# VectorE's arithmetic of gathered expert rows ordered behind the one-hot products, and 92 in place of 100 expert tiles run ahead

## The chip, the cores and the metric

The kernel runs on one core of a Trainium2 chip. The metric is the device time of one execution in microseconds (us); three executions are shown, and the median is what counts. One more execution was recorded by the profiler, and all rows and sums below are of that one.

## What is computed

One decoder layer over 512 tokens of 1024 features: a chunked gating mixer and a sparse attention, merged and added to the input, and then a feed-forward layer of 16384 single-neuron experts (128 x 128 keys). The change touches this last part alone:

```python
sub = jnp.einsum('bshpd,hpnd->bshpn', q, subkeys)       # 8 heads, 2 x 128 keys
s_top, i_top = lax.top_k(sub, PEER_TOPK)                # 16 of each half
...
best, pos = lax.top_k(cand, PEER_TOPK)                  # 16 experts of a head
gate = jax.nn.softmax(best, axis=-1)
...
ub = u_tab[eb]                                          # 128 experts of a token
vb = v_tab[eb]
a = jax.nn.gelu(jnp.einsum('td,ted->te', xb, ub))
return jnp.einsum('te,ted->td', (gb * a).astype(vb.dtype), vb)
```

All arrays are float32.

## The kernel before

The 512 tokens are four blocks of 128. The first three blocks (384 tokens, the **dense** way) are computed against all 16384 experts by matmul, with gates that are zero for the experts a token did not choose. The fourth block (the **sparse** way) fetches the 128 chosen rows of each token from memory.

**Dense, first half.** The u table is 128 tiles of 128 experts. `expert_in` (L652) loads a tile (`load_w`, L81: a DMA of 512 KB on SP's queue into `wraw`, 3 buffers; ScalarE rounds it into `whi`, L86; VectorE takes the rest `wlo`, L87) and makes 24 matmuls into `pa` (8 chunks, three products each, L91 to L93, 384 columns); ScalarE's gelu evacuates it. The first 28 results stay on chip; tiles from `KEPT` = 28 to `AHEAD` are written to memory (`ad`, L660) and read back later (L900).

**Dense, gates.** `choose` (L755) finds each token's experts. For each block, 16 steps of 8 tokens then build the gate matrix out of one-hot products: four VectorE operations of 128x1024 (`jb`, `ib`, `o1`, `o2`, L837 to L840), 16 small matmuls into `pg` (L846), an evacuation by ScalarE into `ch`, and a write to memory (`gd`, L850, one for two steps). There are 48 such steps.

**Dense, second half.** For each of 128 tiles of the v table (L888 on): the tile is loaded like the u tiles, a slice of the gates is read back (`gg`, 1.5 MB for 8 tiles), VectorE multiplies the activations by the gates (`pr`, L904), ScalarE and VectorE split the product (`ph`, `pl`), and 18 matmuls of 512 columns add into six banks `y`.

**Sparse.** `sparse_in` (L672) gathers one chosen u row for each of the 128 tokens (GpSimd issues an indirect DMA of 512 KB into `gt`, L668, **three buffers**), and one VectorE operation (L674) multiplies by the token's features and sums; every 16 of them a gelu and a multiplication make `coef`. `sparse_out` (L681) gathers a v row and VectorE adds it, weighted, to `h2l` (L683). There are 128 of each; a gather can be issued when the VectorE operation three gathers earlier has freed its buffer.

**What sets the order.** The text runs `ahead(1)` (L687) before each one-hot step, an expert tile, and after every second tile a `sparse_in`; when the one-hot steps are through, `ahead(P)` does the tiles up to `AHEAD`. In the last loop `feed()` (L865) puts the rest of the sparse work evenly between the loads. But the order in which an engine executes is not the text's: when the program is built, a scheduler plays it through with durations of its own and lets an instruction go ahead of others on its engine when its operands are ready there. The executed order is fixed from then on, and each engine takes its instructions strictly in that order. `tc.issue_after(x)` forbids the scheduler to put what is inside ahead of `x`.

Of the kernel before, what the change touches and what calls it, by code (L numbers as in the profile page):

```python
# [15 lines left out]
ALU = mybir.AluOpType  # L16
# [44 lines left out]
def kernel(ctx: ExitStack, tc: tile.TileContext, x, pos, cst, wtok, wsm, wcol, wkv, spt,  # L61
                             wab, wo, wq, skt, g1b, g2b, u_rows, ut, v_rows, out, dbg=None):
    nc = tc.nc
    V, G, A, T, SY = nc.vector, nc.gpsimd, nc.scalar, nc.tensor, nc.sync
# [78 lines left out]
    with ExitStack() as c1:  # L143
# [39 lines left out]
        with tc.tile_pool(name="xin", bufs=4, reuse_waits="tile") as xp:  # L183
# [53 lines left out]
            with tc.tile_pool(name="rp", bufs=1) as rp:  # L237
# [38 lines left out]
                for k, p2 in ((a1, 9), (a2, 20)):  # L276
# [4 lines left out]
                    t = tmp()  # L281
                    V.tensor_scalar(t, k, mh, None, ALU.mult)
                    t = reduce(t)
                    t = sub_mul(t, k, -(m - mh))
# [87 lines left out]
        for b in range(NB):  # L372
# [8 lines left out]
            s = m  # L381
# [89 lines left out]
        for b in range(1, NB):  # L471
            s = madd[b]
# [20 lines left out]
        for g in range(4):  # L493
# [8 lines left out]
            t = sc.tile([P, S], F32, name="zt", tag="w", bufs=NW)  # L502
# [69 lines left out]
        h2l = spp.tile([P, D], F32, name="h2l")  # L572
# [8 lines left out]
        for p in range(4, 8):  # L581
            out_tile(p, ybh, ybl)
            for i in (2 * p - 8, 2 * p - 7):
                t = sg[i]
# [11 lines left out]
        hn3 = spp.tile([P, D], F32, name="hn3")  # L596
# [36 lines left out]
    TO = 8  # L633
    NCH = ND // TC
    JG = 8
    AHEAD = 100
    KEPT = 28
    EARLY = 2
    GS = 2.0 ** 15
# [3 lines left out]
    dots = spp.tile([P, P], F32, name="dots")  # L643
    coef = spp.tile([P, P], F32, name="coef")
# [21 lines left out]
    def gather(table, s):  # L666
# [2 lines left out]
                             in_offset=bass.IndirectOffsetOnAxis(ap=eid[:, s:s + 1], axis=0))  # L669
        return t  # L670

    def sparse_in(s):  # L672
        t = gather(u_rows, s)
        V.tensor_tensor_reduce(out=t, in0=t, in1=hn3, scale=1.0, scalar=0.0, op0=ALU.mult, op1=ALU.add,  # L674
                               accum_out=dots[:, s:s + 1])
        if s % PK == PK - 1:
            hs = slice(s - PK + 1, s + 1)
            A.activation(coef[:, hs], dots[:, hs], AF.Gelu_apprx_tanh)
            V.tensor_tensor(coef[:, hs], coef[:, hs], gate3[:, hs], ALU.mult)

    def sparse_out(s):  # L681
        t = gather(v_rows, s)
        V.scalar_tensor_tensor(h2l, t, coef[:, s:s + 1], h2l, ALU.mult, ALU.add)  # L683

    n_in = 0

# [9 lines left out]
    with ExitStack() as c2:  # L696
# [114 lines left out]
        for b in range(NB - 1):  # L811
            ahead(2)
            tr = []
            for n, src in enumerate(choose(b)):
                pt = sm.tile([P, S], F32, name="pgt", tag="sm")
                T.transpose(pt[:, :P], src, ident)
                t = gs.tile([P, P], F32 if n == 2 else F16, name=f"tr{n}")
# [5 lines left out]
            glo = gs.tile([P, P], F16, name="glo")  # L823
            V.tensor_tensor(glo, gT, ghi, ALU.subtract)
            for cc in range(P // TC):
                ch = chp.tile([P, P, TC], F32, name="ch")
                for to in range(0, TC, TO):
# [4 lines left out]
                    def over(a):  # L832
                        return (a[:, t0:t0 + TO].rearrange("p (g u) -> p g u", u=2).unsqueeze(2)
                                .to_broadcast([P, TO // 2, P, 2]))
# [2 lines left out]
                    V.tensor_tensor(jb, iob, over(jT), ALU.is_equal)  # L837
                    V.tensor_tensor(ib, iob, over(iT), ALU.is_equal)
                    V.tensor_tensor(o1, ib, over(ghi), ALU.mult)
                    V.tensor_tensor(o2, ib, over(glo), ALU.mult)  # L840
                    for t4 in range(0, TO, 4):
                        pg = gp.tile([P, 4, P], F32, name="pg")
                        for u in range(4):
# [148 lines left out]
```

## Time and profile before

| what | us |
|---|---|
| three executions | 1598.27, 1598.01, 1592.77 |
| median | 1598.01 |
| the profiled execution | 1593.43 |
| its span, first to last instruction | 1591.7 |
| TensorE busy in it | 1559.4 |
| VectorE busy | 1265.2 |
| ScalarE busy | 657.5 |
| GpSimd busy | 345.4 |

The profiled execution stands 4.6 us below the median of the three. TensorE's mean granted clock is 0.993 of full speed. Instructions of an engine overlap a little at their ends, so a mean duration is slightly more than the step from one start to the next; for matmuls the overlap is large, and the step is what counts. Up to about 450 us the profile shows the mixer and attention and then the query projections; from 530 to 890 us the gates and the expert tiles that run ahead; from there to the end the v tiles with the remaining u tiles.

### The profile page before, as it was taken

To read this page: it belongs to the slowest core of one execution; us is meant where nothing else is said; L and a number is where in the kernel's file an instruction comes from. 1 tells how busy PE (TensorE), PEld (TensorE's weight loads), DVE (VectorE), ACT (ScalarE), POOL (GpSimd) and SP (SyncE) were. 2 spreads that over 40 slices of the span, in tenths; PEclk is the share of its full clock that TensorE was granted. 3 is DMA by queue.
4 is the path that set the end of the run, shared out by engine and by line. 5 is a ranking of instruction groups with operands and counts; after the bars stand their busy time and mean duration, and the time that the engine had idled before them with its cause. 6 is when DMAs were issued, how large, how long until landed. Compare 5 with 4: busy or idle time off the path is not lost.

```text
span 1591.7 us, 22605 instructions
## 1 busy us (share of the span) xinstructions
PE 1559.4 (98%) x8173; PEld 1359.1 (85%) x8173; DVE 1265.2 (79%) x2648; ACT 657.5 (41%) x976; POOL 345.4 (22%) x280
## 2 busy tenths in 40 slices
PE   8998999999999999999999899999999999999998
PEld 6777767888899999899999898888888888888787
DVE  5599945557999999999999567788777788788764
ACT  5453453322335345455567343333333333333232
POOL 0010000000000454333222223343322223334300
PEclk9999999999999999999999999999999999999999
DMA  6211225222223789999999998899999999999862
GB/s 219 80 54 67 93 71 194 93 93 93 80 93 120 256 304 339 330 328 356 365 342 340 369 348 271 304 352 346 361 330 354 351 338 333 328 316 317 274 230 94
DMA packets 160416, 395.01 MB, mean 248 GB/s; under 512 B 12976, under 2 KB 80560, under 8 KB 156720
## 3 DMA queue, kind: packets, MB, share of 16 engines
q1 hardware_dynamic: 109616, 220.01, 39.6%
q0 software_dynamic: 36864, 134.23, 23.7%
q10 hardware_dynamic: 13824, 39.33, 6.4%
q8 instruction: 64, 1.05, 0.3%
q14 instruction: 48, 0.39, 0.1%
HBM read 350.53 MB, written 42.99 MB: 247 GB/s over the span
## 4 chain that ended last, share of the span: by engine, by line
PE 78%; DMA 9%; issue 6%; DVE 3%; POOL 2%; ACT 1%; SPq 0%; POOLq 0%; DVEq 0%; ACTq 0%
PE pa L93 9%; PE pa L91 9%; PE pa L92 9%; PE y L92 7%; PE y L93 7%; PE y L91 7%; DMA gt<-in_v_rows,eid 5%; PE pg L846 3%; POOL gt L668 2%; PE pcol L92 2%; PE pcol L91 2%; PE pcol L93 2%; PE pq L91 2%; PE pq L92 2%; PE pq L93 2%
## 5 line engine op out<-in xcount | busy, mean ns | idle before, releaser
L86 ACT CAST whi<-wraw 128x1024 fp32r<-128x1024 f32 x320 | 334.6, 1051 | 322.1 <-PE pa L92 127.0
L87 DVE TENSOR_TENSOR wlo<-wraw,whi 128x1024 fp32r<-128x1024 f32 x320 | 389.1, 1219 | 88.1 <-ACT whi L86 81.1
L91 PE MATMUL pa<-hh,whi 128*128 128x384 f32 (+2 forms) x1040 | 351.2, 338 | 10.0 <-ACT actd L659 10.0
L93 PE MATMUL pa<-hh,wlo 128*128 128x384 f32 (+2 forms) x1040 | 349.7, 337 | 1.1 <-DVE wlo L87 1.1
L92 PE MATMUL pa<-hl,whi 128*128 128x384 f32 (+2 forms) x1040 | 349.6, 336 | 0.0
L92 PE MATMUL y<-wlo,ph 128*128 128x512 f32 x768 | 302.3, 394 | 4.5 <-DVE wlo L87 4.5
L93 PE MATMUL y<-whi,pl 128*128 128x512 f32 x768 | 300.9, 393 | 0.0
L668 POOL DMA_INDIRECT gt<-in_u_rows,eid x128 | 177.9, 1390 | 527.9 <-DVE dots L674 308.8
L908 ACT CAST ph<-pr 128x384 fp32r<-128x384 f32 x128 | 65.8, 514 | 381.2 <-PE y L92 360.0
L668 POOL DMA_INDIRECT gt<-in_v_rows,eid x128 | 155.3, 1213 | 308.8 <-DVE h2l L683 276.3
L91 PEld LDWEIGHTS pa<-hh,whi 128*128 128x128 f32 x1040 | 196.5, 189 | 15.3 <-ACT actd L659 11.0
L91 PE MATMUL y<-whi,ph 128*128 128x512 f32 x768 | 207.6, 392 | 0.2 <-ACT ph L908 0.2
L93 PEld LDWEIGHTS pa<-hh,wlo 128*128 128x128 f32 x1040 | 196.3, 189 | 6.2 <-DVE wlo L87 2.2
L92 PEld LDWEIGHTS pa<-hl,whi 128*128 128x128 f32 x1040 | 196.6, 189 | 4.2
L683 DVE SCALAR_TENSOR_TENSOR h2l<-gt,coef,h2l 128x1024 f32<-128x1024 f32 x128 | 163.8, 1280 | 27.0 <-DMA gt<-in_v_rows,eid 26.2
L92 PEld LDWEIGHTS y<-wlo,ph 128*128 128x128 f32 x768 | 144.9, 189 | 34.9 <-DVE wlo L87 5.1
L93 PEld LDWEIGHTS y<-whi,pl 128*128 128x128 f32 x768 | 145.0, 189 | 28.4 <-DVE pl L909 0.3
L674 DVE CUSTOM_DVE_ANT_0 gt<-gt,hn 128x1024 f32<-128x1024 f32 x128 | 155.3, 1218 | 17.0 <-DMA gt<-in_u_rows,eid 16.9
L91 PEld LDWEIGHTS y<-whi,ph 128*128 128x128 f32 x768 | 143.7, 188 | 26.9 <-ACT ph L908 0.5
L909 DVE TENSOR_TENSOR pl<-pr,ph 128x384 fp32r<-128x384 f32 x128 | 71.2, 556 | 90.8 <-ACT ph L908 87.2
L848 ACT ACTIVATE ch<-pg 128x512 f32<-128x512 f32 x96 | 96.6, 1112 | 29.5 <-PE pg L846 29.5
L904 DVE TENSOR_TENSOR pr<-act,gg 128x384 f32<-128x384 f32 x128 | 70.7, 554 | 2.1
(304 smaller groups left out, 1930.4 us busy)
## 6 DMA issues: line engine op xcount, KB each, us to landing
wraw<-in_ut SPq DMA_DIRECT2D x128, 512.0 KB, 5.6
wraw<-in_v_rows SPq DMA_DIRECT2D x128, 512.0 KB, 6.6
gd<-ch ACTq DMA_DIRECT2D x24, 1024.0 KB, 6.3
gg<-gd SPq DMA_DIRECT2D x15, 1536.0 KB, 15.1
ad<-actd ACTq DMA_DIRECT2D x72, 192.0 KB, 5.5
act<-ad SPq DMA_DIRECT2D x72, 192.0 KB, 7.3
wraw<-in_wcol SPq DMA_DIRECT2D x20, 512.0 KB, 3.2
wraw<-in_wq SPq DMA_DIRECT2D x16, 512.0 KB, 3.2
```

The lines of the kernel that those rows point to most:

```text
L86: A.copy(hi, raw)
L87: V.tensor_tensor(lo, raw, hi.bitcast(F32), ALU.subtract)
L91: T.matmul(ps, lh, rh, start=start, stop=False)
L92: T.matmul(ps, lh, rl, start=False, stop=False)
L93: return T.matmul(ps, ll, rh, start=False, stop=stop)
L668: G.indirect_dma_start(out=t, out_offset=None, in_=table, in_offset=bass.IndirectOffsetOnAxis(ap=eid[:, s:s + 1], axis=0))
L674: V.tensor_tensor_reduce(out=t, in0=t, in1=hn3, scale=1.0, scalar=0.0, op0=ALU.mult, op1=ALU.add, accum_out=dots[:, s:s + 1])
L683: V.scalar_tensor_tensor(h2l, t, coef[:, s:s + 1], h2l, ALU.mult, ALU.add)
L848: A.activation(ch[:, :, to + t4:to + t4 + 4].rearrange("p i t -> p t i"), pg, AF.Copy, scale=1.0 / GS)
L904: V.tensor_tensor(pr.rearrange("p (c t) -> p c t", c=NCH), acts[j].rearrange("p (c t) -> p c t", c=NCH), gt[:, :, j % JG, :], ALU.mult)
L908: A.copy(ph, pr)
L909: V.tensor_tensor(pl, pr, ph.bitcast(F32), ALU.subtract)
```

## The change

The sparse VectorE operations (`sparse_in`'s product and `sparse_out`'s addition) may no longer be placed ahead of the last one-hot product `o2` that the text has emitted before them. Before the first one-hot step there is none, and they are free. `AHEAD` goes from 100 to 92: 8 expert tiles are done in the last loop instead of in front of it, 8 fewer results go through `ad`, and 4 fewer `sparse_in` stand in the text before the last loop.

```diff
--- before.py
+++ after.py
@@ -633,7 +633,7 @@
     TO = 8
     NCH = ND // TC
     JG = 8
-    AHEAD = 100
+    AHEAD = 92
     KEPT = 28
     EARLY = 2
     GS = 2.0 ** 15
@@ -669,10 +669,17 @@
                              in_offset=bass.IndirectOffsetOnAxis(ap=eid[:, s:s + 1], axis=0))
         return t
 
+    last_v = None
+
+    def paced():
+
+        return tc.issue_after(last_v.ins) if last_v is not None else nullcontext()
+
     def sparse_in(s):
         t = gather(u_rows, s)
-        V.tensor_tensor_reduce(out=t, in0=t, in1=hn3, scale=1.0, scalar=0.0, op0=ALU.mult, op1=ALU.add,
-                               accum_out=dots[:, s:s + 1])
+        with paced():
+            V.tensor_tensor_reduce(out=t, in0=t, in1=hn3, scale=1.0, scalar=0.0, op0=ALU.mult, op1=ALU.add,
+                                   accum_out=dots[:, s:s + 1])
         if s % PK == PK - 1:
             hs = slice(s - PK + 1, s + 1)
             A.activation(coef[:, hs], dots[:, hs], AF.Gelu_apprx_tanh)
@@ -680,7 +687,8 @@
 
     def sparse_out(s):
         t = gather(v_rows, s)
-        V.scalar_tensor_tensor(h2l, t, coef[:, s:s + 1], h2l, ALU.mult, ALU.add)
+        with paced():
+            V.scalar_tensor_tensor(h2l, t, coef[:, s:s + 1], h2l, ALU.mult, ALU.add)
 
     n_in = 0
 
@@ -837,7 +845,7 @@
                     V.tensor_tensor(jb, iob, over(jT), ALU.is_equal)
                     V.tensor_tensor(ib, iob, over(iT), ALU.is_equal)
                     V.tensor_tensor(o1, ib, over(ghi), ALU.mult)
-                    V.tensor_tensor(o2, ib, over(glo), ALU.mult)
+                    last_v = V.tensor_tensor(o2, ib, over(glo), ALU.mult)
                     for t4 in range(0, TO, 4):
                         pg = gp.tile([P, 4, P], F32, name="pg")
                         for u in range(4):
```

What becomes of the order is seen on VectorE's queue. Names: `gt,dots<-gt,hn` is `sparse_in`'s product (with a second row that reads out the sum), `h2l<-gt,coef,h2l` is `sparse_out`'s addition, `wlo` the split of any weight tile, `ib`, `jb` and `o` the one-hot products, the rest of the first place belongs to `choose`; `eid` holds the row numbers for the gathers. Line numbers of the change are 8 higher from L681 on.

The first place: VectorE from the first gathered product on, soon after `eid` is known. Before:

```order
L674 ISA gt,dots<-gt,hn_2653 128x1024
L674 ISA dots 128x1
L781 TENSOR_SCALAR qt_5560<-qa 128x128
L715 MATCH_REPLACE cand<-best,cand 128x64 x3
L87 TENSOR_TENSOR wlo<-wraw,whi 128x1024
L674 ISA gt,dots<-gt,hn_2653 128x1024
L674 ISA dots 128x1
L793 TENSOR_TENSOR eq<-eq 128x128x8
L716 MAX best<-cand 128x8
L674 ISA gt,dots<-gt,hn_2653 128x1024
L674 ISA dots 128x1
```

and with the change:

```order
L681 ISA gt,dots<-gt,hn_2653 128x1024
L681 ISA dots 128x1
L789 TENSOR_SCALAR qt_5560<-qa 128x128
L723 MATCH_REPLACE cand<-best,cand 128x64 x3
L87 TENSOR_TENSOR wlo<-wraw,whi 128x1024
L801 TENSOR_TENSOR eq<-eq 128x128x8
L724 MAX best<-cand 128x8 x5
L788 SCALAR_TENSOR_TENSOR qb<-qa,qb 128x128
L87 TENSOR_TENSOR wlo<-wraw,whi 128x1024
L724 MAX best<-cand 128x8 x3
L801 TENSOR_TENSOR eq<-eq 128x128x4
```

Before, a product follows every two or three rows of `choose`; now one is placed here, and the next comes 57 rows later, after the first `o2`.

The second place: VectorE from the last `o2` on. Before:

```order
L840 TENSOR_TENSOR o_7818<-ib,glo 128x1024
L87 TENSOR_TENSOR wlo<-wraw,whi 128x1024
L674 ISA gt,dots<-gt,hn_2653 128x1024
L674 ISA dots 128x1
L87 TENSOR_TENSOR wlo<-wraw,whi 128x1024
L674 ISA gt,dots<-gt,hn_2653 128x1024
L674 ISA dots 128x1
L87 TENSOR_TENSOR wlo<-wraw,whi 128x1024
L674 ISA gt,dots<-gt,hn_2653 128x1024
```

and with the change:

```order
L848 TENSOR_TENSOR o_7818<-ib,glo 128x1024
L681 ISA gt,dots<-gt,hn_2653 128x1024
L681 ISA dots 128x1
L681 ISA gt,dots<-gt,hn_2653 128x1024
L681 ISA dots 128x1
L87 TENSOR_TENSOR wlo<-wraw,whi 128x1024
L681 ISA gt,dots<-gt,hn_2653 128x1024
L681 ISA dots 128x1
L87 TENSOR_TENSOR wlo<-wraw,whi 128x1024 x2
L681 ISA gt,dots<-gt,hn_2653 128x1024
L681 ISA dots 128x1
```

Before, one product and one `wlo` take turns here; now two products stand together between some of the `wlo`.

The third place: VectorE over the last v tiles. Before:

```order
L904 TENSOR_TENSOR pr<-act,gg 128x384
L87 TENSOR_TENSOR wlo<-wraw,whi 128x1024
L909 TENSOR_TENSOR pl<-pr,ph 128x384
L87 TENSOR_TENSOR wlo<-wraw,whi 128x1024
L909 TENSOR_TENSOR pl<-pr,ph 128x384
L87 TENSOR_TENSOR wlo<-wraw,whi 128x1024 x2
L921 TENSOR_TENSOR hr<-hr,y_0_9432 128x512
```

and with the change:

```order
L691 SCALAR_TENSOR_TENSOR h2l<-gt,coef,h2l 128x1024
L912 TENSOR_TENSOR pr<-act,gg 128x384
L87 TENSOR_TENSOR wlo<-wraw,whi 128x1024
L691 SCALAR_TENSOR_TENSOR h2l<-gt,coef,h2l 128x1024 x2
L917 TENSOR_TENSOR pl<-pr,ph 128x384
L691 SCALAR_TENSOR_TENSOR h2l<-gt,coef,h2l 128x1024
L87 TENSOR_TENSOR wlo<-wraw,whi 128x1024
L912 TENSOR_TENSOR pr<-act,gg 128x384
L691 SCALAR_TENSOR_TENSOR h2l<-gt,coef,h2l 128x1024
L917 TENSOR_TENSOR pl<-pr,ph 128x384
L87 TENSOR_TENSOR wlo<-wraw,whi 128x1024
L917 TENSOR_TENSOR pl<-pr,ph 128x384
```

Before, the last `h2l` addition stood 14 v tiles ahead of the end; now the additions go on until two tiles before it.

Counted over the whole of the queue:

| VectorE's order | products and `wlo` before | with the change |
|---|---|---|
| products ahead of the first `o2` | 22 | 1 |
| products ahead of the 48th `o2` | 84 | 27 |
| `wlo` ahead of the first `o2` | 102 | 95 |
| `wlo` ahead of the 48th `o2` | 157 | 134 |
| products, `wlo` between the 48th `o2` and the first `pl` | 7, 6 | 9, 8 |
| `h2l` additions ahead of the 89th, 113th, 127th `pl` | 83, 126, 128 | 57, 99, 128 |

and on TensorE's queue: u tiles ahead of the last `pg` matmul 89.2 before and 66.0 with the change (884 and 1441 of the `pa` matmuls come after it); u tiles between it and the first `y` 5.8 and 5.0; u tiles between v tiles 89 and 113 6.0 before, and between v tiles 89 and 127 10.2 with the change.

## Rows read from the trace of the kernel before

**Rows 1.** The page's head and its part 1, busy time of the engines.
```profile
span 1591.7 us, 22605 instructions
...
PE 1559.4 (98%) x8173; PEld 1359.1 (85%) x8173; DVE 1265.2 (79%) x2648; ACT 657.5 (41%) x976; POOL 345.4 (22%) x280
```

**Rows 2.** Windows of the whole core, with the columns named in the first line.
```profile
core 0: us, PE busy (x) PEld busy (x) DVE busy (x) ACT busy (x) POOL busy (x), PEclk, DMA share, GB/s
0.00:530.00 530.00, 517.96 (x2495) 430.77 (x2496) 399.31 (x1464) 218.02 (x389) 15.65 (x26) 1.00 0.30 105
530.00:600.00 70.00, 68.93 (x395) 67.50 (x394) 66.91 (x144) 26.84 (x39) 34.76 (x23) 1.00 0.88 306
600.00:890.00 290.00, 286.43 (x2119) 273.24 (x2119) 270.04 (x403) 174.34 (x218) 91.51 (x65) 0.99 0.95 344
890.00:925.00 35.00, 28.21 (x142) 27.07 (x141) 19.27 (x27) 11.84 (x17) 5.80 (x5) 0.90 1.05 372
925.00:1480.00 555.00, 553.97 (x2577) 474.45 (x2576) 441.39 (x531) 195.06 (x271) 184.27 (x151) 1.00 0.94 331
1480.00:1520.00 40.00, 36.29 (x156) 30.43 (x155) 29.57 (x33) 9.30 (x13) 13.38 (x12) 0.91 0.86 295
1520.00:1591.70 71.70, 67.58 (x299) 55.67 (x297) 38.73 (x51) 22.09 (x30) 0.00 (x0) 0.99 0.39 141
```

**Rows 3.** Groups by line, shapes apart: us busy, mean ns of one, idle before.
```profile
L87 DVE TENSOR_TENSOR wlo<-wraw,whi 128x1024 fp32r<-128x1024 f32 x320 | 389.1, 1219 | 88.1 <-ACT whi L86 81.1 <-PE psub L735 4.2 <-issue 2.3
...
L683 DVE SCALAR_TENSOR_TENSOR h2l<-gt,coef,h2l 128x1024 f32<-128x1024 f32 x128 | 163.8, 1280 | 27.0 <-DMA gt<-in_v_rows,eid 26.2
...
L674 DVE CUSTOM_DVE_ANT_0 gt<-gt,hn 128x1024 f32<-128x1024 f32 x128 | 155.3, 1218 | 17.0 <-DMA gt<-in_u_rows,eid 16.9
...
L674 DVE DVE_READ_ACCUMULATOR2_ANT dots<- 128x1 f32 x128 | 10.4, 82 | 0.0
```

**Rows 4.** Windows of TensorE, tile pa alone, then tile y alone.
```profile
480.00:520.00 40.00, 40.00 (x233) 1.00 0.34 119
...
1540.00:1580.00 40.00, 40.00 (x178) 1.00 0.33 120
```

**Rows 5.** The tile pg: the one-hot matmuls' first and last start.
```profile
L846 PE MATMUL pg<-o,jb x768: 217/218/330, 599.7 to 886.4; 128*128 128x128 f16 x192
```

**Rows 6.** Waits from 630 to 655 us: total, times, longest.
```profile
ACT whi L86 <- DMA wraw<-in_ut: 8.0, 2, 4.4
...
PE pa L91 <- ACT actd L659: 2.7, 2, 2.4
```

**Rows 7.** Waits from 870 to 930 us.
```profile
ACT whi L86 <- DMA wraw<-in_ut: 8.5, 1, 8.5
...
PE pa L91 <- ACT actd L659: 6.8, 1, 6.8
```

**Rows 8.** Waits from 1480 to 1520 us.
```profile
DVE h2l L683 <- DMA gt<-in_v_rows,eid: 10.4, 7, 3.9
...
PE y L92 <- DVE wlo L87: 3.7, 1, 3.7
```

**Rows 9.** Waits of the whole span on GpSimd's queue.
```profile
POOL gt L668 <- DVE dots L674: 314.5, 100, 13.7
POOL gt L668 <- DVE h2l L683: 276.3, 102, 8.9
```

**Rows 10.** Windows of GpSimd, the gathers (tile gt) alone.
```profile
1440.00:1480.00 40.00, 17.24 (x14) 1.00 0.90 305
1480.00:1520.00 40.00, 13.38 (x12) 0.91 0.86 295
```

**Rows 11.** DMA issues of the whole span: KB each, median us to landing.
```profile
ad<-actd ACTq DMA_DIRECT2D x72, 192.0 KB, 5.5
gt<-in_v_rows,eid POOLq DMA_INDIRECT x128, 7.3
gg<-gd SPq DMA_DIRECT2D x15, 1536.0 KB, 15.1
```

## The prediction

> **What bounds the kernel now.** The page's head first: TensorE is busy in 1559.4 of 1591.7 us [rows 1], so all that any reordering can win is what is left, 32.3 us, and what the clock loses behind a pause. Next the windows by stage [rows 2], where the reader is to see where these 32.3 us lie: 12.0 ahead of 530 us, 1.1 and 3.6 in the gates' stage (530 to 890), 6.8 at its end (890 to 925), 1.0 in the first 555 us of the v tiles, 3.7 from 1480 to 1520, 4.1 at the end. In the same rows the granted clock shows three places at which TensorE had fallen to its lower level, 1.2 GHz in place of 2.4, after it had paused: a mean of 0.99, 0.90 and 0.91. One minus that, times the window: 2.9, 3.5 and 3.6 us; the first is rounded coarsely (1.5 to 4.4 us fit it), and I count 1.6, near its lower end.
>
> Then the waits, for what ended these pauses. In the stage of the gates [rows 6] and at its end [rows 7] TensorE waits for ScalarE's gelu; ScalarE takes its work strictly in order and stands in front of the rounding of a u tile whose load is late (8.0 and 8.5 us). At the end of the stage that load was issued behind the first gate slice, and such a slice takes 15.1 us to land [rows 11]. At 1490 us TensorE waits for a `wlo` on VectorE, and VectorE stands in front of `h2l` additions whose gathered rows have not landed (10.4 us) [rows 8]. GpSimd in turn waits 314.5 and 276.3 us for VectorE to free one of the three buffers [rows 9]: gathers are a ring in which landing, VectorE's operation and the next issue follow each other.
>
> What counts for the matmuls is the step from start to start. Where TensorE does nothing else, 233 `pa` fit into 40 us and 178 `y` [rows 4]: 0.172 and 0.225 us, so 24 x 0.172 = 4.12 us for a u tile and 18 x 0.225 = 4.04 us for a v tile.
>
> **What the change removes, adds and moves.** It removes 8 round trips through `ad` of 192 KB [rows 11], 3.1 MB in all; at the 331 GB/s of the long stage [rows 2] that is 9.5 us of traffic, none of it on TensorE's path: nothing taken off. If transfers were what the stage waits for, it would be up to -9.5. It adds no instruction. Everything else is moved. VectorE: 84 - 27 = 57 products of 1.218 + 0.082 us and 157 - 134 = 23 `wlo` of 1.219 us [rows 3] leave the stretch ahead of the last one-hot product for the one behind it, 74 + 28 = 102 us. TensorE: 89.2 - 66.0 = 23.2 u tiles, 95.6 us, go the same way. GpSimd's gathers and SP's loads go with them, since each gather waits for the ring and each load for its buffer. As TensorE does the same work in both kernels, the sum is one of stalls, taken place by place. Up to the first product, behind `eid`, VectorE's order is the same, so the first 525 us or so stay.
>
> *Gates.* Between the first and the last `o2`, 62 - 26 = 36 products and 55 - 39 = 16 `wlo` are gone. VectorE had 270.0 of 290 us busy, 93% [rows 2]; it will have 270.0 - 36 x 1.30 - 16 x 1.219 = 203.7 in 290 - 16 x 4.12 = 224, 91%. So VectorE is as full as before, in a shorter stage, and does not become free. The traffic falls: 344 GB/s x 290 us = 99.8 MB, less 52 transfers of 0.524 MB and 16 of 0.197, are 69.4 MB in 224 us, 310 GB/s. The late loads that made this stage's stalls (1.1 + 3.6 + 1.6 = 6.3 us) should be fewer. Between 0 and 6.3 I take half: **-3**.
>
> *The end of the stage.* TensorE's cover between the last one-hot matmul and the first `y` shrinks from 5.8 to 5.0 u tiles, 23.9 to 20.6 us, while VectorE has 9 products and 8 `wlo` to do in place of 7 and 6. In bytes: 13 transfers of 0.524 MB, a gate slice of 1.5 and a gate write of 1.05 are 9.4 MB, at 372 GB/s [rows 2] 25 us; now 11.5 MB, 31 us. The shortfall goes from 1 to 10 us. The bounds are a stall that disappears because the queues are less full when the stage ends (-10.3, that is 6.8 and 3.5 of clock) and one that grows by the difference (+9). The traffic ahead of it speaks for the one and the bytes for the other: **+2**.
>
> *The v tiles.* Here the question is the ring. In 1440 to 1520 us, where it was what TensorE waited for, 26 gathers were issued in 80 us [rows 10], 3.08 us each. From its parts: 7.3 us to land [rows 11] and 1.28 of VectorE [rows 3], for three buffers, 2.86 us. Before, from the 89th to the 113th v tile, 43 additions stood beside 24 x 4.04 + 6.0 x 4.12 = 122 us of TensorE: 123 to 132 us of ring, and TensorE lost 3.7 + 3.6. TensorE has up to two tiles in hand, some 8 us. With the change, from the 89th to the 127th, it is 71 additions beside 38 x 4.04 + 10.2 x 4.12 = 196 us: 203 to 219 us of ring. Less the 8 us in hand, nothing to 15 us are lost, and up to 3.6 of clock with them, in place of the 8.3 us (1.0 + 3.7 + 3.6) lost among the v tiles before: -8 to +10. The ring's parts fit the record before better than the bound rate, since its cover was exceeded by little there and TensorE lost little: near the middle, **+2**. Behind the 127th tile nothing of the sparse work is left, so it hangs over the end of TensorE's work by nothing.
>
> The Trainium skill would have it otherwise: "DMA: Bandwidth & Descriptors", section "Anatomy of one DMA — SWDGE (gpsimd) path", gives a transfer issued from GpSimd a fixed 2.0 us and its bytes at 436 GB/s, by estimate 3.2 us for a gather; the ring would then turn in 1.5 us, and this place would be worth -8.3 rather than +2. The measured landing of 7.3 us is more than twice that, so the sum stays with the row.
>
> Sum: -3 + 2 + 2 = **+1 us** against the profiled execution's own 1593.4, so 1594.4 there. The median of the runs stands 4.6 us above that execution, and I forecast **1599 us** in its terms. A measurement of this kernel can tell some 0.5%, 8 us, from no change; so this is no change.
>
> **The rivals.**
>
> *The ring ends last (slower).* The range is 2.86 to 3.08 us for one turn, and it decides from (196 + 8) / 71 = 2.87 us on, at the very lower end. At 3.08 the v tiles cost +10, and with the longer shortfall at the end of the gates (+9) and the -3 it is +16: 1614 us. For it: the longest stretch of dense gathers before was 122 us, now 196, and gate slices of 15.1 us come every 8 tiles within it. Against it: over the 555 us from 925 on, 151 of GpSimd's issues went by with 1.0 us lost [rows 2]. Chance 0.17.
>
> *Bytes become the bound (slower).* Behind the last one-hot matmul, 98 + 128 gathers (three products' rows are fetched by then) and 184 weight tiles of 0.524 MB (three are loaded) make 215 MB, the gate slices, `ad` and `gd` 44, the last reads and writes 4: 263 MB. Before, that place was at 886.4 us [rows 5], and the rest took 705 us with 884 x 0.172 + 2304 x 0.225 = 670 us of matmuls, so 35 on top; now 1441 x 0.172 + 518 + 35 = 801 us. 263 MB at 331 GB/s [rows 2] are 795. It is a near thing: at 320 GB/s it is 822, +21, so 1619 us. Against it: from 600 to 890 the rate was 344 with hardly a pause, and 372 in the densest window. Chance 0.10.
>
> The same page, section "Specifications", gives a core about 358 GB/s from memory; by estimate 735 us for these bytes, and no bound. The 372 GB/s measured exceeds it, so it is not a limit here.
>
> *The pauses go (faster).* With less traffic ahead of it the pause at 900 us does not arise, and a ring that is spread over more tiles lets the last one go: of 6.3 + 10.3 + 8.3 = 24.9 us the larger part, say 15, comes back: 1583 us; all of it, 1573. For it: each of the three pauses had a late transfer at its start [rows 6 to 8]. The skill's price of a gather would be the part of this case that lies among the v tiles, and nothing more; the landing row gives it no chance apart from it. Against it: the additions are no more evenly spread than before towards the end. Chance 0.24.
>
> That the change does nothing is excluded by the order of both queues.
>
> **How the numbers follow.** No change has 0.49, faster 0.24, slower 0.17 + 0.10 = 0.27. The forecast's own case covers 1590 to 1606 us. The range takes in the typical faster case and the ring's: 1582 to 1616 us, which leaves out the fully faster case and bytes as the bound, some 0.2.
>
> **What would show it.** Right: the last `pg` matmul ends near 886.4 - 95.6 - 3, about 788 us; the windows of the gates' stage show fewer GB/s than 344 with VectorE still above 88%; gathers go on until some 10 us before the end; a pause behind the last `pg` is still there; total idle time of TensorE stays near 32 us. The ring as bound would show as TensorE's waits for `wlo` and `pl` after 1400 us with VectorE waiting for gathered rows; bytes as the bound as a DMA share at 1 over the v tiles and waits from 900 us on. Wrong would be a wait of another kind, above all one of ScalarE's queue on `coef`, or a last `pg` that comes much later than 788 us.

## The result and the profile after

| kernel | runs | median us | ratio to before, 95% interval |
|---|---|---|---|
| before, measured beside it | 4 | 1595.39 | |
| changed | 4 | 1609.59 | 1.0108 (1.0083 to 1.0132) |

The change makes the kernel 1.1% slower. That is inside the range given and outside the case held likeliest, no change. The profiled execution took 1606.08 us, 12.7 more than the one before (1593.43). The page of the changed kernel, its head, the engines' line of part 1 and the chain of waits by engine:

```profile
span 1604.3 us, 22566 instructions
...
PE 1562.5 (97%) x8173; PEld 1357.4 (85%) x8173; DVE 1263.3 (79%) x2648; ACT 657.3 (41%) x976; POOL 376.6 (23%) x280
...
PE 54%; issue 23%; DVE 9%; POOL 8%; DMA 6%; ACT 0%; POOLq 0%; SPq 0%; DVEq 0%
```

TensorE idles 41.8 us where it idled 32.3 [rows 1], and the chain that ended last now runs over TensorE for 54% of the span (78% before); GpSimd's gathers have risen from 2% to 8% and VectorE from 3% to 9%, and 23% (6% before) is "issue", time for which the profile shows no wait. Where the time went is read from the windows, the answer to [rows 2] and with its columns, with boundaries at the new ends of the stages:

```profile
565.00:784.00 219.00, 218.91 (x1734) 203.22 (x1733) 207.70 (x309) 149.30 (x182) 67.16 (x28) 1.00 0.86 304
784.00:845.00 61.00, 50.24 (x246) 46.23 (x245) 35.22 (x51) 20.55 (x30) 13.16 (x10) 0.89 0.95 342
845.00:1040.00 195.00, 194.88 (x988) 177.16 (x986) 143.19 (x210) 68.18 (x97) 75.01 (x60) 1.00 0.93 325
1040.00:1080.00 40.00, 37.13 (x170) 31.96 (x170) 31.13 (x46) 13.36 (x18) 18.70 (x13) 0.96 0.91 317
1080.00:1480.00 400.00, 400.00 (x1864) 343.32 (x1863) 319.90 (x376) 140.95 (x195) 138.53 (x109) 1.00 0.95 335
1480.00:1520.00 40.00, 36.41 (x169) 30.74 (x169) 30.91 (x34) 13.03 (x18) 17.70 (x13) 1.00 0.85 291
1520.00:1560.00 40.00, 35.52 (x157) 29.51 (x156) 30.64 (x34) 9.67 (x14) 17.57 (x14) 0.96 0.83 296
1560.00:1604.30 44.30, 36.11 (x162) 29.52 (x160) 30.18 (x34) 8.88 (x12) 9.92 (x8) 1.00 0.55 196
```

The last one-hot matmul, the answer to [rows 5], starts at 783.8 us; its end was forecast near 788:

```profile
L854 PE MATMUL pg<-o,jb x768: 217/218/235, 565.6 to 783.8; 128*128 128x128 f16 x192
```

Idle time of TensorE plus what the lower clock takes (one minus the granted clock, times the window), stage by stage:

| stage | before | after | difference | forecast |
|---|---|---|---|---|
| gates, to the last `pg` | 1.1 + 3.6 + 1.6 = 6.3 | 0.1 | -6.2 | -3 |
| behind the last `pg` | 6.8 + 3.5 = 10.3 | 10.8 + 6.7 = 17.5 | +7.2 | +2 |
| v tiles to the end, less the last reads and writes (4.1) | 8.3 | 0.1 + 4.5 + 0 + 3.6 + 6.1 + 8.2 - 4.1 = 18.4 | +10.1 | +2 |

The sum is +11.1 of the 12.7 us. The pause behind the last `pg` looks as in [rows 7], only with more of it. Its waits, from 784 to 845 us:

```profile
ACT whi L86 <- DMA wraw<-in_ut: 9.3, 1, 9.3
...
PE pa L91 <- ACT actd L659: 7.2, 1, 7.2
```

And the timeline there, of ScalarE and of SP (start, duration, engine, line, operation; in brackets the idle time ahead and what ended it):

```profile
802.45 1.04 ACT L86 CAST whi<-wraw 128x1024 fp32r<-128x1024 f32 x1 [9.33 <-DMA wraw<-in_ut]
...
783.37 0.38 SPq L891 DMA_DIRECT2D gg<-gd  x1
783.84 21.27 SPq L85 DMA_DIRECT2D wraw<-in_ut  x4
```

The load that ScalarE waits for was issued just behind the first gate slice, at 783.84, and had landed by 802.45. ScalarE stands in front of its rounding, and the gelu that would free TensorE's bank stands behind. The waits from 1480 us to the end answer to [rows 8]:

```profile
DVE h2l L691 <- DMA gt<-in_v_rows,eid: 23.3, 13, 3.7
...
PE y L92 <- DVE wlo L87: 12.3, 7, 2.6
```

It is the picture of before over a longer stretch: TensorE waits 7 times (once before), 12.3 us in all, for a `wlo`, and VectorE stands 23.3 us in front of additions whose rows have not landed. In the windows GpSimd issues 13 and 14 gathers in 40 us there, 3.08 and 2.86 us each.

### The profile page after: what moved, and what is told of

Its sections match the earlier page's. It is cut to its first block, busy times and chain, and to the rows that moved or that the text cites. A ratio compares the mean times of both kernels' runs of the same rounds, so it can differ in the third digit from the quotient of the medians.

```text
span 1604.3 us, 22566 instructions
## 1 busy us (share of the span) xinstructions
PE 1562.5 (97%) x8173; PEld 1357.4 (85%) x8173; DVE 1263.3 (79%) x2648; ACT 657.3 (41%) x976; POOL 376.6 (23%) x280
## 4 chain that ended last, share of the span: by engine, by line
PE 54%; issue 23%; DVE 9%; POOL 8%; DMA 6%; ACT 0%; POOLq 0%; SPq 0%; DVEq 0%
POOL gt L668 8%; PE y L92 7%; PE y L93 7%; PE y L91 6%; DMA gt<-in_v_rows,eid 5%; PE pa L92 3%; PE pa L91 3%; PE pa L93 3%; PE pcol L91 2%; PE pcol L92 2%; PE pcol L93 2%; DVE wlo L87 2%; PE pq L91 2%; PE pq L92 2%; PE pq L93 2%
## 5 line engine op out<-in xcount | busy, mean ns | idle before, releaser
L668 POOL DMA_INDIRECT gt<-in_u_rows,eid x128 | 197.7, 1545 | 591.0 <-DVE dots L681 400.0
L92 PE MATMUL y<-wlo,ph 128*128 128x512 f32 x768 | 303.2, 397 | 13.4 <-DVE wlo L87 13.3
L668 POOL DMA_INDIRECT gt<-in_v_rows,eid x128 | 166.7, 1302 | 278.9 <-DVE h2l L691 241.6
L91 PE MATMUL y<-whi,ph 128*128 128x512 f32 x768 | 224.0, 393 | 5.5 <-ACT ph L916 5.5
L681 DVE CUSTOM_DVE_ANT_0 gt<-gt,hn 128x1024 f32<-128x1024 f32 x128 | 155.5, 1221 | 37.8 <-DMA gt<-in_u_rows,eid 36.5
```

Source lines behind the costliest of these rows:

```text
L91: T.matmul(ps, lh, rh, start=start, stop=False)
L92: T.matmul(ps, lh, rl, start=False, stop=False)
L668: G.indirect_dma_start(out=t, out_offset=None, in_=table, in_offset=bass.IndirectOffsetOnAxis(ap=eid[:, s:s + 1], axis=0))
```

## The experiments

Each kernel differs from the changed one (free92 and ring4b: from the kernel before) only in what is listed; those with four buffers also keep 27 first results on chip in place of 28. Beside these runs the kernel before took 1591.59 us (the first four; median of 19 runs), 1591.13 (the second four; 20) and 1590.53 (the last four; 24). Ratios are to the kernel before as it was measured beside each run. The bands of the first four expectations, and of early1 and hold3, were set from the first result, where the kernel before stood at 1595.39.

| kernel | buffers | ordering | ahead | other | median us | ratio (95%) |
|---|---|---|---|---|---|---|
| before | 3 | free | 100 | | 1590.5 to 1595.4 | 1 |
| changed | 3 | tied | 92 | | 1609.59 | 1.0108 (1.0083 to 1.0132) |
| paced100 | 3 | tied | 100 | | 1603.12 | 1.0070 (1.0048 to 1.0092) |
| free92 | 3 | free | 92 | | 1589.13 | 0.9989 (0.9978 to 1.0001) |
| ring4 | 4 | tied | 92 | | 1589.46 | 0.9983 (0.9969 to 0.9997) |
| ring2 | 2 | tied | 92 | | 1730.27 | 1.0882 (1.0841 to 1.0923) |
| ring4b | 4 | free | 100 | | 1608.05 | 1.0098 (1.0065 to 1.0130) |
| early1 | 3 | tied | 92 | product behind every tile | 1592.56 | 1.0006 (0.9990 to 1.0022) |
| r4gg6 | 4 | tied | 92 | slice behind 3 more loads | 1588.34 | 0.9987 (0.9973 to 1.0001) |
| r4hold | 4 | tied | 92 | products held back | 1577.90 | 0.9918 (0.9888 to 0.9948) |
| r4hold_b | 4 | tied | 92 | the same again | 1576.98 | 0.9917 (0.9893 to 0.9941) |
| hold3 | 3 | tied | 92 | products held back | 1596.66 | 1.0037 (1.0016 to 1.0058) |
| early1hold3 | 3 | tied | 92 | both | 1598.07 | 1.0040 (1.0020 to 1.0059) |
| r4holdearly1 | 4 | tied | 92 | both | 1578.33 | 0.9931 (0.9906 to 0.9955) |

### The two halves of the change

The ordering alone:

```diff
-    AHEAD = 92
+    AHEAD = 100
```

> The change's ordering alone, with 100 tiles run ahead as before. Its order of VectorE has 27 products and 134 `wlo` ahead of the last one-hot product, exactly as in the changed kernel, and 60 u tiles behind it; the ring of gathers is 3 additions later at the end (60 in place of 57 at the 89th v tile, last addition at the 128th tile in place of the 126th). If the ordering is what costs, by a ring of gathers that ends last: 1609 us, 1605 to 1615, TensorE idle some 40 us, gaps of 1.5 to 3 us from 1480 us to the end. If the 8 tiles fewer are what costs (5.0 in place of 5.8 u tiles of cover, more u tiles among the v tiles): about 1596, like the kernel before.

The 8 tiles alone (the kernel before with this one line):

```diff
-    AHEAD = 100
+    AHEAD = 92
```

> The 8 tiles alone, without the ordering. Its order has 84 products and 157 `wlo` ahead of the last one-hot product, exactly as before, and 3.8 in place of 5.8 u tiles between the last one-hot matmul and the first `y`; the additions are 3 further on at the 89th v tile and the last one stands at the 113th in place of the 114th. If the ring of gathers is what costs: as before, 1596 us, 1590 to 1600, with the gaps near 1490 us again and nothing from 1530 on. If the smaller cover at the end of the gates' stage is what costs: up to 2 tiles x 4.12 = 8 us slower than before, 1604, with the pause behind the last `pg` at 15 us or more.

Measured: 1603.12 and 1589.13 us. The ordering costs 0.7%, 2 us below its expected band; the 8 tiles cost nothing. The windows of the ordering alone, then those of the 8 tiles alone:

```profile
784.00:845.00 61.00, 49.87 (x249) 46.11 (x247) 34.33 (x49) 21.08 (x30) 13.18 (x10) 0.89 0.96 340
...
1480.00:1607.00 127.00, 111.90 (x477) 90.92 (x475) 99.55 (x111) 33.43 (x46) 50.38 (x37) 0.95 0.82 281
```

```profile
885.00:925.00 40.00, 29.69 (x154) 27.61 (x152) 23.06 (x35) 13.40 (x20) 7.75 (x7) 0.87 1.05 365
...
1480.00:1585.70 105.70, 101.70 (x471) 86.67 (x470) 53.75 (x67) 30.75 (x43) 4.22 (x3) 1.00 0.44 150
```

With the ordering, 11.1 us idle behind the last `pg` and 15.1 behind 1480 us, near the changed kernel's 10.8 and 16.3 (this profiled execution, 1609.13 us, was the slowest of its four, 6 us above their median). With the 8 tiles alone, the pause behind the last `pg` grows too, from 6.8 us idle and 3.5 of clock [rows 2] to 10.3 and 5.2, and nothing is lost behind 1480 us but the 4.0 us of the last reads and writes. So "the 8 tiles cost nothing" is a balance: what they lose at the end of the gates' stage they win behind 1480 us. Whether the 8 tiles cost something on top of the ordering (1.0108 against 1.0070) stays open: the two intervals overlap, and the two were not measured beside each other.

### The length of the ring

```diff
-    KEPT = 28
+    KEPT = 27
-    gat = ctx.enter_context(tc.tile_pool(name="gat", bufs=3, reuse_waits="tile"))
+    gat = ctx.enter_context(tc.tile_pool(name="gat", bufs=4, reuse_waits="tile"))
```

> The changed kernel with four buffers for gathered rows in place of three, and the room taken from one kept result (27 in place of 28 first u tiles stay on chip, one more goes through `ad`). VectorE's order is nearly the changed kernel's (27 products ahead of the last one-hot product; additions 61, 102, 118 ahead of tiles 89, 113, 121 in place of 57, 99, 115). If the ring's length is what holds the end: the pauses behind 1480 us go (16.3 us idle of TensorE from there to the end falls to 6 to 9), and the time is 1600 us, 1597 to 1604. If the bytes are the limit, four gathers in flight take longer each, 9 to 10 us in place of 7.3, and the time stays at 1607 to 1613.

And two buffers, with the 28 results of the changed kernel:

```diff
-    gat = ctx.enter_context(tc.tile_pool(name="gat", bufs=3, reuse_waits="tile"))
+    gat = ctx.enter_context(tc.tile_pool(name="gat", bufs=2, reuse_waits="tile"))
```

> The changed kernel with two buffers for gathered rows. Ring theory: a turn is (7.3 + 1.28) / 2 = 4.3 us at the landing measured before, and with less in flight perhaps (5.5 + 1.28) / 2 = 3.4; behind the last one-hot product some 229 turns have 820 us, 3.58 us each. So between 10 us lost (3.4 us; only the bunched end suffers) and 160 us (4.3 us): I expect 1650, from 1620 to 1770, with TensorE's waits for `wlo` and `pl` behind VectorE's waits for gathered rows over the whole of the v tiles. If the bytes are the limit, the length of the ring does nothing: 1607 to 1613.

Measured: 1589.46 and 1730.27 us. Four buffers take back all of the loss, 8 us below the band I gave (4 of them because the kernel before, too, took less beside these runs). Two take 80 us more than the 1650 I expected, inside the wide band, near its end for a turn of 4.3 us. VectorE's additions by line (us busy, mean ns of one, idle time ahead and what ended it) in the changed kernel, and then with four buffers:

```profile
L691 DVE SCALAR_TENSOR_TENSOR h2l<-gt,coef,h2l 128x1024 f32<-128x1024 f32 x128 | 163.9, 1281 | 42.5 <-DMA gt<-in_v_rows,eid 41.9
```

```profile
L691 DVE SCALAR_TENSOR_TENSOR h2l<-gt,coef,h2l 128x1024 f32<-128x1024 f32 x128 | 163.8, 1280 | 6.0 <-DMA gt<-in_v_rows,eid 5.3
```

The windows with four buffers:

```profile
785.90:850.00 64.10, 48.82 (x242) 45.30 (x239) 36.36 (x53) 20.59 (x30) 15.95 (x14) 0.87 0.96 345
850.00:925.00 75.00, 75.00 (x397) 70.35 (x396) 52.63 (x77) 25.72 (x38) 29.41 (x22) 1.00 0.92 327
925.00:1480.00 555.00, 555.00 (x2630) 482.19 (x2629) 447.26 (x559) 197.24 (x274) 204.60 (x162) 1.00 0.96 338
1480.00:1520.00 40.00, 40.00 (x188) 34.36 (x187) 36.15 (x39) 13.29 (x19) 16.33 (x15) 1.00 0.94 330
1520.00:1560.00 40.00, 40.00 (x187) 34.31 (x186) 35.05 (x39) 12.36 (x18) 17.65 (x13) 1.00 0.89 321
1560.00:1588.80 28.80, 24.88 (x113) 20.65 (x111) 12.55 (x16) 5.95 (x8) 0.00 (x0) 1.00 0.25 92
```

From 850 us to the end not a single pause is left but the 3.9 us of the last reads and writes: everything that the v tiles lost, in the window from 1040 to 1080 us as well as behind 1480, was the ring (the one result fewer that is kept on chip is the only other difference). In the same windows the traffic is higher than with three buffers (338 against 332 GB/s from 925 to 1480, 330 against 291 from 1480 to 1520), so three buffers had kept the transfers waiting, not the transfers the buffers. Two buffers show the other side:

```profile
792.00:1480.00 688.00, 629.27 (x2909) 541.50 (x2908) 456.17 (x606) 214.89 (x301) 191.13 (x158) 0.96 0.86 294
1480.00:1728.90 248.90, 191.54 (x836) 159.50 (x834) 167.33 (x178) 59.61 (x82) 75.31 (x68) 0.90 0.74 244
```

TensorE idles all through the v tiles while the DMA rate falls to 294 and 244 GB/s. From the last `pg` (its last start is at 791.2 us) to the end 229 gathers took 938 us, 4.1 us each: near the (7.3 + 1.28) / 2 = 4.3 that the rows before give. With this, bytes as the bound over the v tiles are out.

### Fewer additions left for the end

```diff
-    EARLY = 2
+    EARLY = 1
```

> The changed kernel (three buffers) with a sparse product behind every expert tile in place of every second one. Its order has 54 products ahead of the last one-hot product (27 in the changed kernel, 84 before) and 66 additions ahead of the 89th v tile (57). From there to the last addition 62 additions stand beside 34 x 4.04 + 9.7 x 4.12 = 177 us of TensorE, 2.86 us a turn; changed kernel 71 beside 191, 2.70; before 45 beside 126, 2.79; the 8 tiles alone, 42 beside 123, 2.92, which lost nothing behind 1300 us. If it is the ring at the end, the losses behind 1480 us fall to those of before or less (5 to 9 us idle in place of 16.3), and the time is 1600 us, 1595 to 1604. If the ordering as such, by whatever other way, costs: 1606 to 1612.

Measured: 1592.56 us, ratio 1.0006; the loss of the change is gone with three buffers too. It fell 2 us below the band, with the kernel before 4 us lower beside it. The windows behind the last `pg` (820 to 870) and from 1480 on:

```profile
820.00:870.00 50.00, 46.79 (x287) 43.71 (x286) 34.33 (x48) 25.39 (x33) 9.91 (x9) 1.00 1.02 370
...
1480.00:1589.00 109.00, 97.95 (x442) 82.03 (x440) 71.54 (x81) 28.89 (x40) 25.55 (x21) 0.98 0.66 225
```

The end improves less than I expected (11.1 us idle, 16.3 in the changed kernel, 5 to 9 expected), and the pause behind the last `pg` far more: 3.2 us idle at full clock, in place of 10.8 and 6.7. That the same edit also helps there was not in my theory, and it led to the next experiments. The trace shows a part of it: between the last `pg` and the first `y` stand 5.9 u tiles and 6 gathers, in place of 5.0 and 7 in the changed kernel. But the kernel before has 5.8 and 6 there and idles 6.8 us, so these two counts do not explain all.

### Four buffers without the ordering

The kernel before, with the edit of ring4:

> The kernel before with four buffers for gathered rows (27 first results kept instead of 28), no ordering, 100 tiles ahead. Its order has 98 products ahead of the last one-hot product and the last addition at the 101st v tile. If a ring of three is worth only what is lost behind 1480 us (3.7 us of idle TensorE and 3.6 of clock, some of it coming back as more traffic in the gates' stage): 1588 us, 1582 to 1593. If the change itself, with four buffers, is better than the order before with four buffers: 1593 or more, behind the 1589.5 of the changed kernel with four. If both only need the ring: the two are within 4 us of each other.

Measured: 1608.05 us, 1% slower. Of the three expectations the second came true (behind the changed kernel with four buffers), but 15 us above the 1593 that it starts from, and for a reason that none of the three names. Its windows:

```profile
600.00:897.00 297.00, 280.87 (x2060) 265.81 (x2060) 281.97 (x430) 171.71 (x215) 102.68 (x76) 0.99 0.95 346
897.00:980.00 83.00, 70.98 (x357) 65.09 (x356) 53.16 (x77) 28.84 (x41) 23.64 (x19) 0.94 1.00 358
...
1480.00:1607.60 127.60, 123.61 (x556) 103.15 (x555) 60.69 (x80) 39.10 (x54) 0.00 (x0) 1.00 0.41 138
```

and waits from 600 to 897 us, with one of the kernel before, from 600 to 890 us, below them:

```profile
PE pa L91 <- ACT actd L659: 10.1, 12, 2.0
...
ACT whi L86 <- DMA wraw<-in_ut: 8.9, 5, 3.3
```

```profile
ACT whi L86 <- DMA wraw<-in_ut: 13.3, 3, 5.3
```

The end loses nothing (nothing is issued on GpSimd behind 1480 us), but the gates' stage from 600 us on loses 16.1 us, against 3.6 [rows 2], and the pause behind it is 12.0. With a fourth buffer and no ordering the scheduler had put 98 products ahead of the last one-hot product (84 before, 27 in the changed kernel). VectorE is 95% busy in the stage (93% before) and the rate is 346 GB/s (344); TensorE waits 12 times for a gelu. ScalarE's own waits for u loads have not grown (8.9 us, 13.3 before), so later loads are not what is new; whether the fuller VectorE is, by way of ScalarE's order, was not settled. What is shown is that this order loses in this stage; that it does so because more products crowd it is argued. The ring decides which order is better: free or tied with three buffers is 1 against 1.0108, with four it is 1.0098 against 0.9983 (92 tiles ahead where tied, 100 where free).

### The pause behind the last one-hot product

With four buffers it is what is left: 15.3 us idle and 8.3 of clock. Two theories: the gate slice stands ahead of the u loads in SP's queue (B), or the gathers take the bytes (A). For B, the slice is placed behind three more loads; `loads` holds what `load_w` issues:

```diff
-        gt0 = load_g(0)
+        with tc.issue_after(loads[-18].ins):
+            gt0 = load_g(0)
```

> The changed kernel with four buffers, and the first gate slice placed behind three more u loads on SP's queue (the piece of 23 chunks after the loads that stood just behind it). Theory B, its place in the queue makes the pause: the first pause behind the last `pg`, 11.5 us, falls below 4, the second, ahead of the first `y`, is 4 to 8, and the time is 1580 us, 1575 to 1586. Theory A, the bytes of gathers, slice and loads together are too many there: the pause only moves to the first `y` (a sum of 13 to 18 us idle), and the time stays at 1587 to 1592.

For A, the products that follow the last one-hot product are held back on VectorE until the first `pl`, and the gathers with them:

```diff
-        ahead(P)
+        ahead(P, sparse=False)
...
-            V.tensor_tensor(pl, pr, ph.bitcast(F32), ALU.subtract)
+            split = V.tensor_tensor(pl, pr, ph.bitcast(F32), ALU.subtract)
+            if j == 0:
+                last_v = split
```

> The changed kernel with four buffers, and the sparse products that would follow the last one-hot product held back on VectorE until the first v tile's `pl` is done (in its order 27 in place of 38 products ahead of it; additions 54, 94 and 111 in place of 61, 102 and 118 ahead of tiles 89, 113, 121). With four buffers alone the pause behind the last `pg` is 16.0 us idle and 8 of clock. Theory A, the gathers that the ring lets loose there take the bytes from the u loads: 11 gathers of 0.524 MB fewer are 17 us at 345 GB/s, the pause falls to 5 us or less and the clock with it, and the time is 1575 us, 1570 to 1582. Theory B, the first gate slice stands ahead of the u loads in SP's queue and gathers don't matter: the pause stays at 12 to 17 us, and the time is 1589, up to 1597 if the later additions cost something at the end.

Measured: 1588.34 (0.1% below before, within its noise) and 1577.90 us. With the slice later, the window, and the wait of TensorE in it:

```profile
786.00:850.00 64.00, 49.27 (x251) 45.25 (x250) 37.55 (x54) 21.48 (x31) 16.42 (x13) 0.89 1.00 348
```

```profile
ACT whi L88 <- DMA wraw<-in_v_rows: 15.8, 1, 15.8
...
PE y L93 <- ACT whi L88: 13.8, 1, 13.8
```

The pause only moved to the first `y`: 14.7 us idle in place of 15.3. Theory B, as it was put on record, falls: the slice's place does not set the length of the pause. That the slice itself costs nothing is not shown: the load now waited for is the first v tile's, which in this order stands right behind the slice, and the slice's bytes count in theory A as well. With the products held back:

```profile
788.00:850.00 62.00, 58.44 (x299) 53.71 (x298) 39.51 (x56) 22.08 (x33) 17.24 (x12) 0.97 0.99 350
...
1480.00:1575.00 95.00, 91.31 (x422) 77.56 (x420) 81.39 (x89) 27.70 (x39) 43.49 (x31) 1.00 0.84 300
```

The pause shrinks to 3.6 us idle and 1.9 of clock, at the same 350 GB/s. Up to the first load behind the gate slice, the transfers on SP's queue are in the same order in ring4 and r4hold. That load in ring4, in SP's and ScalarE's timeline, and below it the gathers from 785 to 810 us (tile `gt`: count, ns least/median/most, first and last start):

```profile
785.68 25.64 SPq L85 DMA_DIRECT2D wraw<-in_ut  x4
...
808.67 1.04 ACT L86 CAST whi<-wraw 128x1024 fp32r<-128x1024 f32 x1 [14.62 <-DMA wraw<-in_ut]
```

```profile
L668 POOL DMA_INDIRECT gt<-in_u_rows,eid x6: 939/940/1985, 783.9 to 800.4; - x6
```

and in r4hold:

```profile
784.64 7.30 SPq L85 DMA_DIRECT2D wraw<-in_ut  x3
...
797.09 1.05 ACT L86 CAST whi<-wraw 128x1024 fp32r<-128x1024 f32 x1 [6.38 <-DMA wraw<-in_ut]
```

```profile
L668 POOL DMA_INDIRECT gt<-in_u_rows,eid x3: 1307/1677/1982, 805.0 to 809.3; - x3
```

Without these six gathers (and one more, issued at 781.9), the load takes 12.5 us from issue to ScalarE's use instead of 23.0. Behind it the scheduler also put three v loads ahead of the fourth u load, so the rest of the shorter pause can't be put down to bytes alone. More traces bear on it. In four kernels 5.0 u tiles stand between the last `pg` and the first `y`; the windows of just that stretch, with TensorE's busy time and GpSimd's gathers (the count behind POOL's), in hold3 (described below), ring2, the changed kernel and ring4:

```profile
785.70:808.40 22.70, 21.20 (x123) 20.88 (x123) 10.13 (x14) 10.53 (x15) 2.01 (x2) 1.00 0.97 346
```

```profile
791.40:820.20 28.80, 23.26 (x122) 22.62 (x121) 13.97 (x20) 9.59 (x15) 6.18 (x5) 0.88 0.98 351
```

```profile
784.00:818.20 34.20, 23.72 (x122) 23.08 (x120) 15.34 (x23) 10.56 (x16) 8.60 (x7) 0.85 0.92 340
```

```profile
786.10:824.70 38.60, 23.36 (x121) 22.72 (x120) 17.90 (x26) 10.99 (x17) 10.97 (x9) 0.82 0.93 328
```

With 2, 5, 7 and 9 gathers TensorE idles 1.5, 5.5, 10.5 and 15.2 us.

### The hold with three buffers, and the best kernel

The hold in the changed kernel, as above but with three buffers and 28 results kept:

> The changed kernel with its three buffers, and the sparse products held back between the last one-hot product and the first v tile's `pl`. With four buffers this took the pause behind the last `pg` from 16.0 us idle and 8 of clock to 3.7 and 2. Here the pause should go alike, from 10.8 idle and 6.4 of clock to about 3 and 2, -12 us. But the ring has 5 more additions in its last stretch (52 in place of 57 ahead of the 89th v tile, 76 beside some 199 us, 2.62 us a turn against 2.70), so the losses behind 1480 us grow: at 3.0 us a turn by 76 x 3.0 - 199 = 29 less 71 x 3.0 - 191 = 22, +7 with some clock. Together 1603 us, 1597 to 1608, and the loss at the end is the largest of all kernels with three buffers. If what holds the end is not the ring, the time falls by the pause alone: 1597 or less.

The same with `EARLY = 1`:

> Three buffers, a product behind every expert tile, and the products held back between the last one-hot product and the first `pl`. Without the hold this kernel took 1592.6 us, with 3.5 us idle behind the last `pg` and 7 us or so more than the last reads and writes need behind 1470 us. The hold has little to win there, 0 to 3 us, and costs 2 additions of the ring's room at the end (64 in place of 66 ahead of the 89th v tile), 0 to 6 us. 1594 us, 1588 to 1600. If the hold helps whatever the ring does: 1588 or less.

With four buffers, the hold and `EARLY = 1`:

> Four buffers, the hold, and a product behind every expert tile: 54 in place of 27 products ahead of the last one-hot product. Without that, four buffers and the hold took 1577.9 us with 3.7 us lost behind the last `pg` and nothing at the end. If the gates' stage bears 54 products (as it did with three buffers, some 3 us idle there), nothing is left to win: 1578 us, 1575 to 1582. If more gathers in the gates' stage cost something whatever the ring (four buffers with 98 free products lost 19 us there), it is 1583 or more.

And r4hold once more, unchanged:

> The changed kernel with four buffers and the hold once more, in more rounds: 1578 us, 1575 to 1582, 0.8% (0.5 to 1.1) faster than the kernel before.

Measured: 1596.66, 1598.07, 1578.33 and 1576.98 us. For hold3:

```profile
788.00:850.00 62.00, 60.50 (x325) 57.04 (x324) 40.61 (x57) 23.62 (x35) 14.99 (x12) 1.00 1.01 358
...
1480.00:1520.00 40.00, 37.98 (x175) 31.76 (x174) 34.79 (x38) 12.93 (x19) 19.77 (x15) 1.00 0.87 308
1520.00:1560.00 40.00, 35.69 (x156) 29.10 (x155) 31.02 (x35) 10.32 (x15) 15.88 (x14) 0.96 0.87 299
1560.00:1588.90 28.90, 21.47 (x93) 16.88 (x92) 21.67 (x24) 4.48 (x6) 8.28 (x7) 1.00 0.69 235
```

The pause goes with three buffers too, to 1.5 us idle at full clock, and the end still loses: 13.8 us idle behind 1480 us, some 4 of it for the last reads and writes. The 7 us more that I expected at the end are not there; the ring turned in 40 / 15 = 2.67 us from 1480 to 1520, faster than the 2.86 to 3.08 I had counted on. This profiled execution (1590.66 us) was the fastest of its ten, 6 us below their median, so a part of the expected loss may lie in the others. The median, 1596.66, lies just below the band, where I had put "not the ring"; but the kernel before was 5 us lower beside it too, and the ratio, 1.0037 of 1595.39, is 1601, inside the band. So this run does not decide; ring4 does. Nor is its loss at the end the largest with three buffers, as I expected: the changed kernel idles 16.3 us there. early1hold3 is within its band: the hold has nothing to win there (1.0040, without it 1.0006). r4holdearly1 is as expected as well: no better than r4hold, since nothing is left at the end to be relieved.

The best kernel is the changed one with a fourth buffer and the held products: 1577 us, 0.8% (0.6 to 1.1) faster than before. Of the 21.9 us that TensorE still idles in r4hold (1575.3 less 1553.4), 13 lie ahead of 530 us, 4 behind the last `pg` and 4 at the last reads and writes.

## Why the prediction was wrong where it was

*The gates* (-3 forecast, -6.2 measured). The mechanism was right: with fewer gathers the traffic falls (304 GB/s, 310 forecast; 344 before), VectorE stays as full (207.7 of 219 us, 95%; 91% forecast), and the stall goes. I took half of it; all of it went. ring4b, with more products there and 16.1 us idle, points the same way.

*The end of the stage* (+2 forecast, +7.2 measured). The two bounds were -10.3 and +9, and I let the lighter traffic ahead of the place speak against the bytes in it. The shortfall decided, and the price of +9 was near. It has two parts, as in the prediction: from the last `pg` to the first `y` there are 7 gathers in place of 6, and 5.0 u tiles of cover in place of 5.8. The gathers matter: r4hold and hold3 take most of the pause away by holding the products back a little longer, moving the slice does not. The cover matters too: with the 8 tiles alone it is 3.8 tiles beside the 6 gathers of before, and the pause is 10.3 + 5.2 us. How the +7.2 divides between the two was not separated.

*The v tiles* (+2 forecast, +10.1 measured). This is the term that was furthest off. The mechanism was right, and the bounds were -8 and +10, worked out from a turn of 2.86 to 3.08 us; the rows after give 2.86 and 3.08. The step that went wrong is "near the middle", argued from the small loss of the kernel before. By the same count that loss was small because only 45 additions were left for the last stretch there; with 71 at 2.70 us of TensorE's time each (counted to the last addition; the prediction has 196 / 71 = 2.76), less than any turn of the range, the whole stretch has to lose. TensorE's time for each addition left sorts the runs only roughly, so the count gives the direction and not the size. Idle time and clock lost behind 1480 us, less the last reads and writes: nothing at 2.92 us (free92), 9 at 2.86 (early1), 7 at 2.79 (before), 14 at 2.70 (changed), 11 at 2.62 (hold3). The Trainium skill, "DMA: Bandwidth & Descriptors", section "Anatomy of one DMA — SWDGE (gpsimd) path", would have had the ring turn in 1.5 us by estimate; with three buffers no window shown has a turn under 2.6.

*The rivals.* "The ring ends last" came true in mechanism, place and size: +16 forecast for it, against the 12.7 of the profiles, with its main signs (waits for `wlo` behind 1480 us, VectorE in front of unlanded rows; no wait of TensorE for `pl` shows). It had a chance of 0.17, less than its arithmetic deserved, since its point of decision, 2.87 us, lay at the lower end of the range of the turn. "Bytes become the bound" was wrong over the v tiles: the rate rises with four buffers and falls with two. "The pauses go" was right for one of the three places.

*The signs.* The last `pg`, the rate, VectorE's share and the pause behind the last `pg` were as forecast. TensorE's idle time was not (41.8, forecast 32), nor the last gather: it came 26 us ahead of the end, at 1578.1, not 10.

*The baseline.* The forecast was made against a median of 1598.01; more runs put the kernel before at 1590.5 to 1595.4. In ratios the forecast was 1.0006 and the range ended at 1616 / 1598.01 = 1.0113, so the measured 1.0108 lies just inside, and only because the range was drawn to take in the ring's case; the sum itself missed.

## What to carry to other kernels

A ring of buffers has a turn (landing plus use, over the number of buffers), and work that is moved to the end of a kernel must leave it that much time per item; where the count says it doesn't, believe the count and not the calm record of a kernel that had fewer items left. When an order keeps background transfers out of one stage, look at what is needed at its end, and try holding them a little longer. Buffers and order have to be tried together: a fourth buffer alone cost 1.0% and the ordering alone 0.7%, both together with a hold and 92 tiles gained 0.8%.

## What was not expected of the hardware

For the length of the pause, the place of a transfer in its own queue mattered less than what the other queue had in flight: putting a slice of 1.5 MB behind three more u loads changed the pause from 15.3 to 14.7 us (and moved the late load to the first v tile), while six gathers on GpSimd's queue went with 23.0 in place of 12.5 us for one 512 KB load on SP's. And a fourth buffer for the gathers, with the free order, made the kernel slower, though the rate in the gates' stage hardly rose (346 GB/s, 344 before).
